# Products of ones on TensorE before the data arrive, later loads for three small tables, and the sum of squares on VectorE in a decoder layer

## The chip, the cores and the metric

The kernel runs on one core of one Trainium2 chip. The metric is device time in microseconds (us) of one execution. A core has TensorE (PE: matrix products, with its weight loads listed apart as PEld), VectorE (DVE), ScalarE (ACT), GpSimd (POOL) and SyncE (SP, which here only issues transfers). Each engine works through its own list of instructions in order; an instruction that waits for another engine holds up everything behind it on its own engine.

## The reference, cut to what matters

One layer of a decoder, for a prompt of 512 tokens and eight single sample tokens. What the opening computes is this part:

```python
def rmsnorm(x, g):
    xf = xf * lax.rsqrt(jnp.mean(xf * xf, axis=-1, keepdims=True) + EPS)
    return xf * g
u = rmsnorm(x, g_mix) @ w_in
qk, conv_new = short_conv(u[..., :2 * M], conv_buf, w_conv, b_conv)
gates = u[..., G0:G0 + 2 * M_HEADS] + b_gate
ig = gates[..., :M_HEADS]
lf = jax.nn.log_sigmoid(gates[..., M_HEADS:])
```

Behind it come four mLSTM heads and four retention heads, an output projection, a cross-attention with four heads over 256 memory tokens, a SwiGLU feed-forward part and a last norm. All arithmetic is float32.

## The kernel before, in words

All 520 tokens (512 and 8) are worked on together, features on the 128 partitions: X holds eight blocks (k = 0 to 7) of 128 features by 520 tokens. A float32 product is made of three faster ones: an operand x is split into hi (x rounded, by ScalarE) and lo (x minus hi, by VectorE or GpSimd), and hi*hi, hi*lo and lo*hi are summed. `split` does this for activations (lines 191 to 195), `wload` for a chunk of weights (line 208 hi on ScalarE, line 209 lo; the set LO_ON_POOL names the chunks whose lo GpSimd makes, among them chunks 2 and 4). `mm_k` (line 223) issues the six products (three times two halves of 260 tokens) of one block k.

The opening works as the blocks of X arrive. The transfers that SP issues are, in order: the gate weights graw, X blocks 0 and 1, weight chunk 0, X blocks 2 and 3, chunk 1, X blocks 4 to 7, the table vec, the constants cst, then chunk after chunk. GpSimd issues the gate bias bg, the state m0 and, after it has cleared the tile, the selectors sel. For each block k ScalarE makes A hi (line 194) and the square of X (line 340; block 5's square is GpSimd's, line 338), VectorE makes A lo (line 195), and GpSimd adds the squares of blocks 0 to 4 (line 342); VectorE adds the rest into ssq (line 353). TensorE adds the gates' columns pg (line 345, four products a block) and the first query block pcv with weight chunk 0; behind that the first key block, also named pcv, with chunk 1. When ssq is there, TensorE sums it over the partitions (nrm, line 285), and `rsqrt_rows` makes the norm's factor r_bc (lines 273 to 278) on ScalarE and VectorE. The products were made from the tokens without the norm, and r_bc is multiplied in when they are read: up (lines 508 to 510), vm (line 532, from ppl, the value block, made with chunk 2), gu (line 400).

Behind the opening the mixer runs its blocks query, key, value of one head after the other, each of 48 products into one of two PSUM buffers, with the conv (cv, line 518) on VectorE. Between them run the gates: gl and gu from pg, transposes pgt (line 406), VectorE's gt, u, ng (lines 412 to 428), transposes pig and plf (line 435), the scans m_r and b_r (lines 439 and 444), transposes pc (line 462), and pG, a product with BG (lines 455 and 465). GpSimd fetches two tables cosr and sinr, multiplies each by r_bc (lines 779 and 780) and makes the lo of chunk 4.

The code is not the order of the instructions. A scheduler (`schedule_with_timeline_sim=True`) simulates the program while it is built and places every engine's instructions by that, so an edit in one place can move instructions elsewhere. In the changed file the lines from the edit on have numbers that differ by one to four.

Of the kernel before, what the change touches and what calls it, by code (L numbers as in the profile page):

```python
# [13 lines left out]
AF = mybir.ActivationFunctionType  # L14
ALU = mybir.AluOpType
# [8 lines left out]
P = 128  # L24
D = 1024
KB = 8
# [15 lines left out]
PAST = 4096  # L42
NEG = -1e30
LOG_EXP = "natural_log_exp_and_others"
RSQRT_SEED = float(0x5F3759DF)


# [93 lines left out]
def decoder_step(ctx: ExitStack, tc: tile.TileContext, i: dict, o: list):  # L141
    nc = tc.nc
    pe, act, dve, pool, sp = nc.tensor, nc.scalar, nc.vector, nc.gpsimd, nc.sync
# [21 lines left out]
    def ps1(name):  # L165
        return psums[-1].tile([P, 512], F32, tag="msc", name=name)

    X = main.tile([P, KB, N], F32, name="X")
# [4 lines left out]
    ssq = main.tile([P, N], F32, name="ssq")  # L173
    cst = ctab.tile([P, C_W], F32, name="cst")
    sel = ctab.tile([P, 12 * P], F32R, name="sel")
    ones = main.tile([P, P], F32, name="ones")
# [134 lines left out]
    pool.memset(gw.bitcast(F32), 0.0)  # L311
    bg = ctab.tile([P, 8], F32, name="bg")
    m0 = ctab.tile([NS, 4], F32, name="m0")
    pool.dma_start(bg, i["b_gate"].broadcast_to([P, 8]))
    pool.dma_start(m0, i["state_mlstm_m"][0])
    sp.dma_start(graw, i["w_g8"])
    for k0, k1 in ((0, 1), (1, 2)):
        sp.dma_start(X[:, k0:k1], i["x"][:, k0:k1])
# [5 lines left out]
    sp.dma_start(vec, i["vec"])  # L324
    sp.dma_start(cst, i["cst"])
    pool.memset(sel.bitcast(F32), 0.0)
    pool.dma_start(sel[:40], i["sel"][:40])
    dve.memset(ones, 1.0)
    dve.memset(eps_c, EPS)
    split(gw[:, :, :36], gw[:, :, 64:], graw[:, :, :36])  # L330
    pg, pq0 = ps2("pg"), ps2("pcv")
# [1 line left out]
    sq = []  # L333
    for k in range(KB):
        split(A[:, 0, k], A[:, 1, k], X[:, k], scale=graw[:, k, 36:37])
        sq.append(p0.tile([P, N], F32, tag="sq", name="sq0"))
        if k == 5:
            pool.tensor_tensor(sq[k], X[:, k], X[:, k], ALU.mult)
        else:
            act.activation(sq[k], X[:, k], AF.Square)  # L340
        if 0 < k < 5:
            pool.tensor_tensor(sq[0], sq[0], sq[k], ALU.add)
        for m, s in ((100, 0), (36, 1))[:: 1 if k < KB - 1 else -1]:
            for a in range(2):
                pe.matmul(
                    pg[:m, a, :H2], gw[:, k, :m], A[:, s, k, a * H2 : (a + 1) * H2],
                    start=k == 0 and s == 0, stop=k == KB - 1 and s == 0,
                )
        mm_k(pq0, w0[0], w0[1], A, k, k, k == 0, k == KB - 1)
        if k >= 6:  # L350
            mm_k(pk0, w1[0], w1[1], A, k - 6, k - 6, k == 6, False)
    for k in range(5, KB):
        dve.tensor_tensor(ssq if k == KB - 1 else sq[k + 1], sq[k], sq[k + 1] if k < KB - 1 else sq[0], ALU.add)
    norm_rows(p0)
    for k in range(2, KB):
        mm_k(pk0, w1[0], w1[1], A, k, k, False, k == KB - 1)
# [7 lines left out]
    with ExitStack() as mx:  # L364
# [136 lines left out]
        def conv_block(kb, dst, ps=None):  # L501
            ps = ps or proj(A, "pcv")
            up = tm("up")
            L0 = 3 + T
            pool.memset(up[:, 0:3], 0.0)
            sview = up[:, L0 : L0 + 4 * NS].rearrange("p (b j) -> p b j", j=4)
            pool.tensor_copy(sview[:, :, 0:3], vec[:, kb, V_BUF : V_BUF + 24].rearrange("p (b j) -> p b j", j=3))
            dve.tensor_tensor(up[:, 3 : 3 + H2], ps[:, 0, :H2], r_bc[:, :H2], ALU.mult)
            dve.tensor_tensor(up[:, 3 + H2 : L0], ps[:, 1, : T - H2], r_bc[:, H2:T], ALU.mult)
            dve.tensor_tensor(sview[:, :, 3], ps[:, 1, T - H2 : H2], r_bc[:, T:], ALU.mult)  # L510
            pool.tensor_copy(cu[:, kb, 0:3], up[:, T : T + 3])
            pool.tensor_copy(cu[:, kb, 3:].rearrange("p (b j) -> p b j", j=3), sview[:, :, 1:4])
            LO = T + 3 + 4 * (NS - 1) + 1
            wc = lambda j: vec[:, kb, V_WC + j : V_WC + j + 1]
            cv = tm("cv")
            act.activation(cv[:, :LO], up[:, 0:LO], AF.Identity, bias=vec[:, kb, V_BC : V_BC + 1], scale=wc(0))
            for j in range(1, 4):
                dve.scalar_tensor_tensor(cv[:, :LO], up[:, j : j + LO], wc(j), cv[:, :LO], ALU.mult, ALU.add)  # L518

            th = tm("th")  # L520
            act.activation(th[:, :LO], cv[:, :LO], AF.Tanh)
            if kb < 4:
                dve.scalar_tensor_tensor(dst[:, :T], th[:, :T], 1.0, cv[:, :T], ALU.add, ALU.mult)
            else:
                pool.tensor_scalar(dst[:, :T], th[:, :T], 1.0, None, ALU.add)
                pool.tensor_tensor(dst[:, :T], dst[:, :T], cv[:, :T], ALU.mult)
            dve.scalar_tensor_tensor(dst[:, T:], th[:, T + 3 : LO : 4], 1.0, cv[:, T + 3 : LO : 4], ALU.add, ALU.mult)
            step()
# [239 lines left out]
        for h in range(4):  # L768
            q, k, v = qkv_tiles(f"m{h}")
# [16 lines left out]
        for h in range(4):  # L786
            q, k, v = qkv_tiles(f"r{h}")
# [416 lines left out]
    for f in range(PLAIN, FB):  # L1204
# [7 lines left out]
        for j, (out, (wh, wl), (xh, xl)) in enumerate(zip(ps, ops, xs)):  # L1212
            for k in range(4):
                for w, x in ((wh, xh), (wh, xl), (wl, xh)):
                    pe.matmul(  # L1215
                        out, w[:, k * P : (k + 1) * P], x[:, k * H2 : (k + 1) * H2],
                        start=k == 0 and w is wh and x is xh, stop=k == 3 and w is wl,
# [31 lines left out]
    for obs in ((0, 1), *((ob,) for ob in range(2, KB - 1))):  # L1249
        pss = [ps2("pfd") for _ in obs]  # L1250
        for k0 in range(0, FB, KB):
            for ps in pss:
                hi, lo = W.get()
                for k in range(k0, min(k0 + KB, FB)):
                    for w, s in ((hi, 0), (hi, 1), (lo, 0)):
                        for a in range(2):
                            pe.matmul(  # L1257
                                ps[:, a, :H2], w[:, k - k0], ff(s, k, slice(a * H2, (a + 1) * H2)),
                                start=k == 0 and w is hi and s == 0, stop=k == FB - 1 and w is lo,
# [26 lines left out]
    for n0, n in ((0, H2), (H2, N - H2)):  # L1286
        ts = slice(n0, n0 + n)
        ps = ps2("pfd")[:, 0, :n]
        for k0 in range(0, FB, KB):
# [3 lines left out]
            for k in range(min(KB, FB - k0)):  # L1293
                for w, s in ((hi, 0), (hi, 1), (lo, 0)):
                    pe.matmul(
                        ps, w[:, k], ff(s, k0 + k, ts),
                        start=k0 + k == 0 and w is hi and s == 0, stop=k0 + k == FB - 1 and w is lo,
# [74 lines left out]
```

## Time and profile before

| | us |
|---|---|
| three runs | 882.13, 884.52, 888.44 |
| their median | 884.52 |
| the profiled execution | 884.46 |
| its span, first to last instruction | 882.7 |

So 1.8 us of the profiled execution lie outside the span. Times in the views count from the span's start. "Busy" is the time in which an engine executes; a mean or a start is taken from one profiled execution. In a row of the timeline, the bracket at the end tells how long the engine was idle before it and what ended that.

### The profile page before, as it was taken

To read this page: it belongs to the slowest core of one execution; us is meant where nothing else is said; L and a number is where in the kernel's file an instruction comes from. 1 tells how busy PE (TensorE), PEld (TensorE's weight loads), DVE (VectorE), ACT (ScalarE), POOL (GpSimd) and SP (SyncE) were. 2 spreads that over 40 slices of the span, in tenths; PEclk is the share of its full clock that TensorE was granted. 3 is DMA by queue.
4 is the path that set the end of the run, shared out by engine and by line. 5 is a ranking of instruction groups with operands and counts; after the bars stand their busy time and mean duration, and the time that the engine had idled before them with its cause. 6 is when DMAs were issued, how large, how long until landed. Compare 5 with 4: busy or idle time off the path is not lost.

```text
span 882.7 us, 16987 instructions
## 1 busy us (share of the span) xinstructions
PE 838.9 (95%) x6707; PEld 821.9 (93%) x6707; DVE 673.3 (76%) x1509; ACT 397.4 (45%) x791; POOL 182.4 (21%) x188
## 2 busy tenths in 40 slices
PE   6999999999999999999999889999999997999994
PEld 5989989999999999889999879999999997999994
DVE  5899999877786678867888897999999997222224
ACT  5455435444546354355443554554445554222221
POOL 5544432221024301424323300000000000010011
PEclk9999999999999999999999989999999998999997
DMA  8333223334235336784764112223332232233213
GB/s 270 98 97 124 83 96 121 123 100 133 94 144 195 118 129 217 254 283 135 223 215 133 66 66 73 97 96 115 122 101 96 97 120 66 84 105 94 90 43 98
DMA packets 34600, 110.56 MB, mean 125 GB/s; under 512 B 4000, under 2 KB 8480, under 8 KB 34264
## 3 DMA queue, kind: packets, MB, share of 16 engines
q1 hardware_dynamic: 28752, 96.06, 33.9%
q0 software_dynamic: 3616, 12.34, 3.9%
q10 hardware_dynamic: 2152, 1.08, 0.5%
q8 instruction: 53, 0.87, 0.4%
q14 instruction: 27, 0.22, 0.1%
HBM read 100.38 MB, written 9.07 MB: 124 GB/s over the span
## 4 chain that ended last, share of the span: by engine, by line
PE 76%; DVE 15%; DMA 3%; issue 2%; ACT 2%; POOL 1%; SPq 0%; DVEq 0%; ACTq 0%; POOLq 0%
PE pfd L1257 13%; PE pfa L1215 6%; PE pfb L1215 6%; PE pcq L223 5%; PE pgt L223 4%; PE pwc L223 4%; PE ppl L223 4%; PE pfg L223 3%; PE pfc L1215 3%; PE pwo L223 3%; PE pfe L1215 3%; PE prp L223 3%; PE pfd L1215 3%; PE pfu L223 2%; DVE cv L518 2%
## 5 line engine op out<-in xcount | busy, mean ns | idle before, releaser
L208 ACT CAST whi<-wraw 128x1024 fp32r<-128x1024 f32 (+1 forms) x104 | 107.2, 1032 | 185.4 <-PE pfd L1257 69.6
L209 DVE TENSOR_TENSOR wlo<-wraw,whi 128x1024 fp32r<-128x1024 f32 (+1 forms) x85 | 108.9, 1282 | 74.9 <-ACT whi L208 72.9
L302 POOL TENSOR_TENSOR ssq<-ssq,sq 128x520 f32<-128x520 f32 x18 | 29.3, 1628 | 371.8 <-ACT sq L301 366.6
L191 ACT CAST qhi<-wsum 128x512 fp32r<-128x512 f32 x72 | 42.9, 619 | 54.1 <-DVE wsum L1175 45.7
L1257 PE MATMUL pfd<-TT,whi 128*128 128x260 f32 x392 | 62.8, 282 | 0.0
L209 POOL TENSOR_TENSOR wlo<-wraw,whi 128x1024 fp32r<-128x1024 f32 x19 | 46.0, 2419 | 67.7 <-ACT whi L208 62.6
L1215 PE MATMUL pfa<-TT,qhi 128*128 128x260 f32 x288 | 53.8, 284 | 0.0
L1257 PEld LDWEIGHTS pfd<-TT,whi 128*128 128x128 f32 x392 | 53.7, 188 | 0.0
L1215 PE MATMUL pfb<-TT,qhi 128*128 128x260 f32 x288 | 53.0, 283 | 0.0
L192 DVE TENSOR_TENSOR qlo<-wsum,qhi 128x512 fp32r<-128x512 f32 x72 | 47.9, 687 | 0.0
L223 PE MATMUL pwc<-B,whi 128*128 128x260 f32 x256 | 43.8, 287 | 3.6 <-DVE X L291 3.0
L223 PE MATMUL ppl<-A,whi 128*128 128x260 f32 x256 | 46.4, 295 | 0.6 <-DVE up L510 0.6
L223 PE MATMUL pcv<-A,whi 128*128 128x260 f32 x256 | 45.6, 294 | 1.1 <-ACT whi L208 1.1
L1215 PEld LDWEIGHTS pfb<-TT,qhi 128*128 128x128 f32 x288 | 44.5, 188 | 0.0
L1215 PEld LDWEIGHTS pfa<-TT,qhi 128*128 128x128 f32 x288 | 44.4, 188 | 0.0
L223 PE MATMUL pgt<-A,whi 128*128 128x260 f32 x256 | 44.0, 287 | 0.0
L223 PE MATMUL prp<-A,whi 128*128 128x260 f32 x256 | 43.8, 287 | 0.0
L1257 PE MATMUL pfd<-A,whi 128*128 128x260 f32 x224 | 37.3, 290 | 6.0 <-DVE gu L1226 6.0
L223 PE MATMUL pcq<-A,whi 128*128 128x260 f32 x256 | 42.0, 283 | 0.0
L1215 PE MATMUL pfa<-TT,qlo 128*128 128x260 f32 x144 | 40.9, 284 | 0.6 <-DVE qlo L192 0.6
L223 PE MATMUL pwo<-B,whi 128*128 128x260 f32 x256 | 41.3, 283 | 0.0
L1215 PE MATMUL pfb<-TT,qlo 128*128 128x260 f32 x144 | 40.8, 283 | 0.0
(435 smaller groups left out, 2625.4 us busy)
## 6 DMA issues: line engine op xcount, KB each, us to landing
wraw<-in_weights_dram SPq DMA_DIRECT2D x132, 512.0 KB, 3.7
kv<-in_cache_k_dram SPq DMA_DIRECT2D x16, 512.0 KB, 4.3
kv<-in_cache_v_dram SPq DMA_DIRECT2D x16, 512.0 KB, 4.3
wraw<-in_weights_dram SPq DMA_DIRECT2D x8, 384.0 KB, 3.1
X<-in_x_dram SPq DMA_DIRECT2D x2, 1040.0 KB, 6.0
Cs<-in_state_C_dram POOLq DMA_DIRECT2D x4, 512.0 KB, 5.1
out_dram<-Cs POOLq DMA_DIRECT2D x4, 512.0 KB, 3.4
Ss<-in_state_S_dram POOLq DMA_DIRECT2D x4, 512.0 KB, 3.9
```

Source lines behind the costliest of these rows:

```text
L191: act.copy(hi, src)
L192: dve.tensor_tensor(lo, src, hi.bitcast(F32), ALU.subtract)
L208: act.copy(hi[:, :n], raw[:, :n])
L209: (pool if index in LO_ON_POOL else dve).tensor_tensor(lo[:, :n], raw[:, :n], hi[:, :n].bitcast(F32), ALU.subtract)
L223: pe.matmul(ps[:m, a, :H2], w[:, k, c0 : c0 + m], x[:, s, xk, a * H2 : (a + 1) * H2], start=first and w is hi and s == 0, stop=last and w ...
L302: (dve if ob == KB - 1 else pool).tensor_tensor(ssq, ssq, s, ALU.add)
L518: dve.scalar_tensor_tensor(cv[:, :LO], up[:, j : j + LO], wc(j), cv[:, :LO], ALU.mult, ALU.add)
L1215: pe.matmul(out, w[:, k * P : (k + 1) * P], x[:, k * H2 : (k + 1) * H2], start=k == 0 and w is wh and x is xh, stop=k == 3 and w is wl,)
L1257: pe.matmul(ps[:, a, :H2], w[:, k - k0], ff(s, k, slice(a * H2, (a + 1) * H2)), start=k == 0 and w is hi and s == 0, stop=k == FB - 1 and ...
```

## The change

It puts ten products of a 128x128 tile of ones with itself at the head of TensorE's work (nothing reads the result), for which the tile of ones is filled first on VectorE. It moves the loads of bg and m0 from GpSimd to SP, behind cst, and the load of sel to GpSimd's work on the first conv block. It gives block 5's square to ScalarE and all seven additions of squares to VectorE, in a running sum as the squares come, so that GpSimd has none.

```diff
--- before.py
+++ after.py
@@ -42,6 +42,7 @@
 PAST = 4096
 NEG = -1e30
 LOG_EXP = "natural_log_exp_and_others"
+WARM = 10
 RSQRT_SEED = float(0x5F3759DF)
 
 
@@ -311,8 +312,10 @@
     pool.memset(gw.bitcast(F32), 0.0)
     bg = ctab.tile([P, 8], F32, name="bg")
     m0 = ctab.tile([NS, 4], F32, name="m0")
-    pool.dma_start(bg, i["b_gate"].broadcast_to([P, 8]))
-    pool.dma_start(m0, i["state_mlstm_m"][0])
+    dve.memset(ones, 1.0)
+    warm = ps1("warm")[:, :P]
+    for _ in range(WARM):
+        pe.matmul(warm, ones, ones, start=True, stop=True)
     sp.dma_start(graw, i["w_g8"])
     for k0, k1 in ((0, 1), (1, 2)):
         sp.dma_start(X[:, k0:k1], i["x"][:, k0:k1])
@@ -324,8 +327,8 @@
     sp.dma_start(vec, i["vec"])
     sp.dma_start(cst, i["cst"])
     pool.memset(sel.bitcast(F32), 0.0)
-    pool.dma_start(sel[:40], i["sel"][:40])
-    dve.memset(ones, 1.0)
+    sp.dma_start(bg, i["b_gate"].broadcast_to([P, 8]))
+    sp.dma_start(m0, i["state_mlstm_m"][0])
     dve.memset(eps_c, EPS)
     split(gw[:, :, :36], gw[:, :, 64:], graw[:, :, :36])
     pg, pq0 = ps2("pg"), ps2("pcv")
@@ -334,12 +337,9 @@
     for k in range(KB):
         split(A[:, 0, k], A[:, 1, k], X[:, k], scale=graw[:, k, 36:37])
         sq.append(p0.tile([P, N], F32, tag="sq", name="sq0"))
-        if k == 5:
-            pool.tensor_tensor(sq[k], X[:, k], X[:, k], ALU.mult)
-        else:
-            act.activation(sq[k], X[:, k], AF.Square)
-        if 0 < k < 5:
-            pool.tensor_tensor(sq[0], sq[0], sq[k], ALU.add)
+        act.activation(sq[k], X[:, k], AF.Square)
+        if k:
+            dve.tensor_tensor(ssq if k == KB - 1 else sq[0], sq[0], sq[k], ALU.add)
         for m, s in ((100, 0), (36, 1))[:: 1 if k < KB - 1 else -1]:
             for a in range(2):
                 pe.matmul(
@@ -349,8 +349,6 @@
         mm_k(pq0, w0[0], w0[1], A, k, k, k == 0, k == KB - 1)
         if k >= 6:
             mm_k(pk0, w1[0], w1[1], A, k - 6, k - 6, k == 6, False)
-    for k in range(5, KB):
-        dve.tensor_tensor(ssq if k == KB - 1 else sq[k + 1], sq[k], sq[k + 1] if k < KB - 1 else sq[0], ALU.add)
     norm_rows(p0)
     for k in range(2, KB):
         mm_k(pk0, w1[0], w1[1], A, k, k, False, k == KB - 1)
@@ -509,6 +507,8 @@
             dve.tensor_tensor(up[:, 3 + H2 : L0], ps[:, 1, : T - H2], r_bc[:, H2:T], ALU.mult)
             dve.tensor_tensor(sview[:, :, 3], ps[:, 1, T - H2 : H2], r_bc[:, T:], ALU.mult)
             pool.tensor_copy(cu[:, kb, 0:3], up[:, T : T + 3])
+            if kb == 0:
+                tc.keep_in_program_order(pool.dma_start(sel[:40], i["sel"][:40]))
             pool.tensor_copy(cu[:, kb, 3:].rearrange("p (b j) -> p b j", j=3), sview[:, :, 1:4])
             LO = T + 3 + 4 * (NS - 1) + 1
             wc = lambda j: vec[:, kb, V_WC + j : V_WC + j + 1]
```

What the scheduler makes of it differs from the order before over the opening and the whole mixer. Three places follow.

TensorE where pg ends and the norm's sum nrm stands. Before, 86 products precede and include the last of pg and 93 precede nrm:

```order
L345 MATMUL pg<-A,gw 36x260 x2
L345 MATMUL pg<-A,gw 100x260 x2
L223 MATMUL pcv<-A,whi 128x260 x4
L223 MATMUL pcv<-A,wlo 128x260 x2
L223 MATMUL pcv<-A,whi 128x260
L285 MATMUL nrm<-ssq,ones 128x260 x2
L223 MATMUL pcv<-A,whi 128x260 x3
L223 MATMUL pcv<-A,wlo 128x260 x2
```

Now it is 111 and 115, the ten products of ones not counted:

```order
L345 MATMUL pg<-A,gw 36x260 x2
L345 MATMUL pg<-A,gw 100x260 x2
L224 MATMUL pcv<-A,whi 128x260 x2
L224 MATMUL pcv<-A,wlo 128x260 x2
L286 MATMUL nrm<-ssq,ones 128x260 x2
L224 MATMUL pcv<-A,wlo 128x260
L224 MATMUL pcv<-A,whi 128x260 x4
L224 MATMUL pcv<-A,wlo 128x260 x2
L224 MATMUL pcv<-A,whi 128x260 x4
L224 MATMUL pcv<-A,wlo 128x260 x2
L224 MATMUL ppl<-A,whi 128x260 x4
L224 MATMUL ppl<-A,wlo 128x260 x2
```

More of the key block's products moved ahead of pg's end and of nrm; 13 of them are left behind nrm, where 35 were.

TensorE where the gates' transposes pgt stand among the 48 products of ppl. Before, after 24 of them, and 75 products lie between pgt and pig:

```order
L223 MATMUL ppl<-A,whi 128x260 x4
L223 MATMUL ppl<-A,wlo 128x260 x2
L406 MATMUL pgt<-cst,gu 128x36 x4
L406 MATMUL pgt<-cst,gu 8x36
L223 MATMUL ppl<-A,whi 128x260 x4
L223 MATMUL ppl<-A,wlo 128x260 x2
```

Now after all 48, and 52 products lie between pgt and pig:

```order
L224 MATMUL ppl<-A,whi 128x260 x4
L224 MATMUL ppl<-A,wlo 128x260 x2
L404 MATMUL pgt<-cst,gu 128x36 x4
L404 MATMUL pgt<-cst,gu 8x36
L224 MATMUL pcv<-A,whi 128x260 x4
L224 MATMUL pcv<-A,wlo 128x260 x2
```

The transposes moved back by 24 products, while pig stays at its place (234 products precede it before, 235 now). Further on, pc moved from 287 to 285, and pG from 318 to 295, so that 2 products lie between pc and pG where 23 lay.

GpSimd around the two tables that it multiplies by r_bc. Before:

```order
L511 COPY cu<-up 128x3
L779 TENSOR_TENSOR cosr<-cosr,r_bc 128x520
L780 TENSOR_TENSOR sinr<-sinr,r_bc 128x520
L512 COPY cu<-up 128x24
L209 TENSOR_TENSOR wlo<-wraw,whi 128x1024
```

Now:

```order
L509 COPY cu<-up 128x3
L511 DMA sel<-in_sel_dram 40x1536
L779 TENSOR_TENSOR cosr<-cosr,r_bc 128x520
L210 TENSOR_TENSOR wlo<-wraw,whi 128x1024
L780 TENSOR_TENSOR sinr<-sinr,r_bc 128x520
```

The issue of sel came in ahead, and the lo of chunk 4 moved between the two tables. On VectorE the lo of chunk 3 moved from behind up into the middle of the norm's factor, and vm from behind the gates' first operations to ahead of gt.

## Rows read from the trace of the kernel before

**Rows 1.** The page's first line.
```profile
span 882.7 us, 16987 instructions
```

**Rows 2.** Chain that ended last, 0 to 60 us: start, us, what.
```profile
2.60 8.40 DMA X<-in_x_dram
...
12.56 2.17 PE pcv L223 x10
...
24.05 0.88 PE nrm L285 x4
24.94 4.18 PE pcv L223 x35
...
31.99 0.41 PE pgt L406 x5
...
33.40 2.71 DVE u L422
...
38.41 2.28 DVE u L427
```

**Rows 3.** Timeline of TensorE, 0 to 14 us: start, us, instruction, idle before.
```profile
5.03 1.44 PE L345 MATMUL pg<-A,gw 128*100 128x260 f32 x4 [5.03 <-ACT A L194]
7.40 1.45 PE L345 MATMUL pg<-A,gw 128*100 128x260 f32 x4 [0.93 <-ACT A L194]
9.99 1.24 PE L223 MATMUL pcv<-A,whi 128*128 128x260 f32 x4 [1.14 <-ACT whi L208]
11.81 0.76 PE L345 MATMUL pg<-A,gw 128*100 128x260 f32 x2 [0.58 <-ACT A L194]
```

**Rows 4.** Timeline of TensorE, 30 to 60 us.
```profile
42.31 0.60 PE L435 MATMUL pig<-cst,gt 128*4 128x128 f32 x4 [0.74 <-DVE lm L474]
...
49.89 0.22 PE L462 MATMUL pc<-cst,b_r 4*128 4x4 f32 x1 [1.15 <-DVE b_r L444]
...
51.14 1.21 PE L223 MATMUL ppl<-A,whi 128*128 128x260 f32 x4 [0.60 <-DVE up L510]
```

**Rows 5.** Busy us by stretch: length, PE, PEld, DVE, ACT, POOL, granted clock, DMA share, GB/s.
```profile
11.00:14.00 3.00, 2.42 (x12) 2.20 (x11) 2.03 (x3) 2.85 (x5) 1.49 (x2) 1.00 1.04 344
...
48.00:51.00 3.00, 1.40 (x15) 1.10 (x13) 3.00 (x8) 0.66 (x1) 1.51 (x1) 1.00 0.49 164
51.00:54.00 3.00, 2.86 (x13) 2.89 (x14) 3.00 (x8) 2.41 (x4) 2.03 (x4) 0.52 0.00 0
...
60.00:100.00 40.00, 38.35 (x317) 37.51 (x317) 38.33 (x98) 19.78 (x56) 22.51 (x28) 1.00 0.30 101
```

**Rows 6.** Transfers, 9 to 12 us: total, and the packets of GpSimd's queue.
```profile
DMA packets 208, 0.78 MB, mean 259 GB/s; under 512 B 36, under 2 KB 36, under 8 KB 208
...
q0 software_dynamic: 54, 0.21, 31.0%
```

**Rows 7.** Transfers, 13 to 16 us: total.
```profile
DMA packets 416, 1.24 MB, mean 412 GB/s; under 512 B 47, under 2 KB 175, under 8 KB 416
```

**Rows 8.** Transfers issued from 0 to 20 us: KB, median us to landing.
```profile
sel<-in_sel_dram POOLq DMA_DIRECT2D x1, 240.0 KB, 8.4
```

**Rows 9.** Timeline of ScalarE, 7 to 27 us.
```profile
8.90 1.04 ACT L208 CAST whi<-wraw 128x1024 fp32r<-128x1024 f32 x1 [1.02 <-DMA wraw<-in_weights_dram]
...
23.24 0.59 ACT L398 COPY gl<-pg 36x520 f32<-36x520 f32 x1 [4.25 <-PE pg L345]
```

**Rows 10.** Timeline of all engines, 0 to 60 us: VectorE's sum of squares.
```profile
22.63 0.70 DVE L353 TENSOR_TENSOR ssq<-sq,sq 128x520 f32<-128x520 f32 x1
```

**Rows 11.** Timeline of GpSimd, 0 to 110 us.
```profile
12.43 3.02 POOL L342 TENSOR_TENSOR sq<-sq,sq 128x520 f32<-128x520 f32 x2 [3.14 <-ACT sq L340]
...
24.86 2.40 POOL L209 TENSOR_TENSOR wlo<-wraw,whi 128x1024 fp32r<-128x1024 f32 x1 [5.68 <-ACT whi L208]
...
33.47 1.31 POOL L779 TENSOR_TENSOR cosr<-cosr,r_bc 128x520 f32<-128x520 f32 x1
34.75 1.29 POOL L780 TENSOR_TENSOR sinr<-sinr,r_bc 128x520 f32<-128x520 f32 x1
```

## The prediction

> **What bounds the kernel now.** I read the chain that ended last first, for the opening: it runs over the landing of X blocks 2 and 3 at 11.00 us (2.60 + 8.40) and from there over TensorE without a gap until the norm's sum nrm at 24.05, the key block behind it and the transposes pgt at 31.99; then over VectorE, with two of its tiny operations (u, 128x20) standing at 2.71 and 2.28 us [rows 2]. So up to 11 us the opening waits for data, then TensorE's amount of work sets the time, and from 32 us on VectorE does. The pace of TensorE comes from the same rows: ten products of 260 columns in 2.17 us at 12.56, 0.217 us each, which is the level of 1.2 GHz; 35 in 4.18 us at 24.94, 0.119 us each, the level of 2.4 GHz. The column of the granted clock reads 1.00 in 11 to 14 us as well [rows 5], against that pace, so in the opening I go by the pace. Second, TensorE's timeline: before 11.81 it does four products, waits 0.93 us, four more, waits 1.14, four more, waits 0.58 [rows 3]. Third, its waits later on: 0.74 us at pig, 1.15 at pc, 0.60 at the next ppl [rows 4]; behind these two last ones the granted clock is 0.52, the 1.2 GHz level, in 51 to 54 us [rows 5]. From 60 to 100 us VectorE is busy 38.33 of 40 us [rows 5], so what it is late with at 60 us stays late.
>
> **The change part by part**, against the profiled execution (884.46 us, 0.06 below the median of the three runs; the span 882.7 lies in it [rows 1]).
>
> *Products of ones.* A product of float32 with 260 columns takes 0.44 us at the full level (nrm, four records for two products, 0.88 us [rows 2]); one of 128 columns is 0.44 x 128 / 260 = 0.22, at the half level 0.43, ten of them 4.3 us. They start when the tile of ones is filled, about 1 us into the span, and end near 5.3; the first products on data began at 5.03 [rows 3], so these come at most 0.3 us later, hidden by the wait behind them. Do they leave the clock at 2.4 GHz for the stretch after 11 us? Between them and 11 us lie the same gaps as before, longer ones if the products run at the full pace. The nearest case in the trace: waits of 1.15 and 0.60 us with eight tiny transposes between them, and the half level from 51 us [rows 4, 5]. The opening has three such gaps in a row, so I take it that the clock is back at 1.2 GHz when the work gets dense, and count 0 for the ten products; the other end is rival A.
>
> The Trainium skill, TensorE: Matmul & The Clock Gate (Rules for kernel authors), advises warming up with matmuls and makes only longer idle gaps than these responsible for a falling clock. By that the sum would be rival A's; the fall at 51 us, behind gaps of 1.15 and 0.60 us, speaks against it, so I follow the row.
>
> *Loads.* sel is 240 KB, in flight 8.4 us [rows 8]. With its packets under way the transfers moved 259 GB/s, of which GpSimd's queue 0.21 MB, in 9 to 12 us, and 412 GB/s without it in 13 to 16 [rows 6, 7]. SP's queue thus got 0.57 MB in 3 us, which takes 1.4 us at 412: 1.6 us lost, about 1.2 of it before X blocks 2 and 3 were there at 11.00. They come at about 9.8. ScalarE is in the hi of chunk 0 until 9.94 (8.90 + 1.04 [rows 9]); before, TensorE's product came 0.81 us after the landing (11.81 - 11.00 [rows 2, 3]), now 0.81 after 9.94: 10.75, 1.06 us earlier. At 0.217 us that is 5 products of lead, worth 5 x 0.119 = 0.6 us. Bounds: 0 (the transfers stay as late) to 1.06 (all at half pace). bg and m0 are needed at gt, 20 us after they can land; the two issues delay only chunk 2, whose hi stands behind gl on ScalarE.
>
> The Trainium skill, DMA: Bandwidth & Descriptors (Issuing engines are not separate DMA queues), says that transfers of all issuers interleave on the same engines. By that alone sel costs its bytes, 0.24 MB / 412 GB/s = 0.6 us, and the product would come at 11.2; rows 6 show more than that.
>
> *Squares.* VectorE gets four additions more, 4 x 0.70 = 2.8 us [rows 10], ScalarE one square; GpSimd's five operations go, and with them their hold on VectorE. Before, ssq was ready at 23.33 (22.63 + 0.70) and nrm began at 24.05 [rows 2, 10]. I cost this at 0, since TensorE now comes to nrm 2.0 us later (next step): that cover of 2.7 us hides even the whole 2.8 but 0.1. Without it the cost lies between -1 and +2.8.
>
> *Order of TensorE's products.* This is the part that costs. 115 products stand ahead of nrm, 93 before: 22 x 0.119 = 2.6, less the lead of 0.6: nrm at 24.05 + 2.0 = 26.05. The end of pg moves by 25 products: 3.0 - 0.6 = 2.4, so gl, at 23.24 before [rows 9], begins at 25.6. Chunk 2's lo hangs on gl through ScalarE's order (gl, hi, then GpSimd's lo): before it ended at 27.26 (24.86 + 2.40 [rows 11]), 4.0 us behind gl's start; now at 29.65. TensorE does nrm until 26.95, its 13 products until 28.5, four of ppl until 29.0, and waits 0.65 us, where there was no wait; 44 more, 5.25 us, end at 34.9. There pgt stands now: 34.9 to 35.3, before 31.99 to 32.40. The norm's factor is no later than that: from nrm's end (24.94) to pgt it took at most 7.05 us, with chunk 3's lo (1024 columns; 520 take 0.70 [rows 10], so some 1.4) that is 35.4 at the latest, half a microsecond behind TensorE at most, and I take 34.9. The gates begin 2.9 us later.
>
> *Gates.* From pgt's end to pig it took 42.31 - 32.40 = 9.9 us [rows 2, 4]. 4.6 of these are the two u (2.71 and 2.28) beyond some 0.2 us each, my estimate for 20 columns where 520 take 0.70; both stood while GpSimd worked (cosr and sinr without a break, 33.47 to 36.04 [rows 11]). Without any such hold it is 5.3, with vm (0.7) ahead of gt 6.0; with both holds 10.6. TensorE has 52 products, 6.2 us, to do in between (75, 8.9, before). So its wait at pig is 0 to 4.4 us. In the new order the lo of chunk 4 and sinr follow each other on GpSimd, 2.4 + 1.3 = 3.7 us; that pair is like cosr and sinr, which held VectorE for all of their time but the start: I take 2.9. Chain 8.9, pig at 44.2, before 42.31: +1.9, a wait of 2.7 us.
>
> *After that.* The scans stand ahead of the convs on VectorE, so pc does not wait (-1.15); but pG comes 2 products behind pc and waits for BG, and the next ppl for up, which now stands behind both. I take these waits and the fall of the clock there as equal to before: 0, with ends at -3.2 (1.15 + 0.60 saved, and the 1.4 us that the 0.52 of 51 to 54 us costs) and +3. Over the rest of the mixer rows change places too; no row prices that, and I give it 0, plus or minus 2.
>
> Sum: 884.46 + 1.9 = 886.4; since the clock may rise somewhat sooner after an earlier start, I say 886.0.
>
> **Rivals.** A, faster: the clock stays at 2.4 GHz from the products of ones on. Then from 10.75 the 93 products left of the 115 take 11.1 us: nrm at 21.9, 2.1 us earlier than before; chunk 2's lo at 25.4 (gl at 21.4), pgt's end at 31.2, pig at 31.2 + 8.9 = 40.1, 2.2 us earlier; 882.3, and with the waits and the fall at 51 us gone (-3.2) 879. I say 881. For it: the order fits such a pace, nrm meeting ssq; against it: the fall in rows 5. B, slower: the wait at pig is so long that the clock falls there. It decides once VectorE is held over both GpSimd operations and the wait passes some 3 us: pig at 35.3 + 10.6 = 45.9 instead of 42.31 (+3.6), 1.4 for the half level behind it, and the +3 at pG and ppl: 892.5. For it: the 2.71 us of u; against it: the two additions at 12.43 took 3.02 us where cosr and sinr took 2.57 [rows 11], as if VectorE had come in between them. C, the change does nothing in the end: TensorE gets as much from the freed VectorE as the later pg costs, and the sum stays at 884.5.
>
> **How the numbers follow.** Forecast 0.42, A 0.25, B 0.13, C 0.20. A measurement of this kernel tells 1% from no change, 8.8 us: below 875.7 there is only A with luck in the mixer (0.03), above 893.3 only B with bad luck (0.05), so 0.92 lie within. The range goes from A's lower end, 879, to 891.5, a little short of B; the forecast's own is 883 to 889.
>
> **What would show it.** Right: products at 0.217 us apart still at 12 to 14 us; the X blocks landing near 9.8; nrm near 26 with VectorE idle ahead of gl; pgt near 35; a wait of TensorE at pig of 2 us or more, none at pc, one at pG. Wrong: a pace of 0.119 from 11 us on, nrm near 22, no wait at pig.

## The result, and the profile after

The kernel after takes 897.31 us in the median of six executions (894.14 to 897.68), the kernel before 885.16 in the same comparison (882.13 to 888.44, six): ratio 1.013, 95% interval 1.0103 to 1.0157, so 11.5 us or 1.3% slower. The forecast was 886.0, and its range ended at 891.5. The profiled execution took 896.97 us; its span, against [rows 1]:

```profile
span 895.1 us, 17026 instructions
```

TensorE's timeline of the kernel after (start, us, instruction, in brackets the idle time before it and what ended it), with what answers to [rows 3, 4] and two places behind them:

```profile
1.06 4.63 PE L318 MATMUL warm<-ones 128*128 128x128 f32 x20 [1.06 <-DVE eps_c L332]
5.35 1.58 PE L345 MATMUL pg<-A,gw 128*100 128x260 f32 x6
...
9.80 1.23 PE L224 MATMUL pcv<-A,whi 128*128 128x260 f32 x4 [2.13 <-ACT whi L209]
10.84 0.69 PE L345 MATMUL pg<-A,gw 128*100 128x260 f32 x2
...
24.18 1.04 PE L286 MATMUL nrm<-ssq,ones 128*128 128x260 f32 x4
...
27.96 0.51 PE L224 MATMUL ppl<-A,wlo 128*128 128x260 f32 x2 [0.69 <-POOL wlo L210]
...
33.40 0.47 PE L404 MATMUL pgt<-cst,gu 36*128 36x36 f32 x5
...
44.28 1.01 PE L433 MATMUL pig<-cst,gt 128*4 128x128 f32 x4 [3.97 <-DVE lm L472]
...
53.41 0.40 PE L463 MATMUL pG<-BG,ones 4*128 4x32 f32 x2 [0.69 <-DVE BG L453]
...
100.68 0.33 PE L651 MATMUL ph<-cst,hs 128*128 128x128 f32 x1 [1.83 <-DVE hs L645]
...
294.38 0.70 PE L847 MATMUL pmn<-msq,ones 128*128 128x256 f32 x2 [1.55 <-POOL msq L844]
```

Against before, the norm's sum nrm is 0.3 us later (24.18 - 23.89), pgt 1.5 (33.40 - 31.92) and pig 2.0 (44.28 - 42.31 [rows 4]), which is the shift that was forecast for pig. The wait at pig is 3.97 us instead of 0.74. At ph, the transposes near 98 us, before waits 0.71 us; after waits 0.99 us at the first of them (98.39) and another 1.83 us at the second, the one shown. Busy time by stretch in the same profile (length, busy us and instructions of TensorE, its weight loads, VectorE, ScalarE, GpSimd, then the granted clock, the share of the DMA engines, GB/s), against [rows 5]:

```profile
6.50:9.50 3.00, 0.86 (x4) 0.34 (x4) 1.30 (x2) 1.22 (x2) 0.00 (x0) 1.00 0.99 365
10.00:13.00 3.00, 3.00 (x14) 2.96 (x15) 3.00 (x5) 3.00 (x5) 0.00 (x0) 0.50 1.04 421
13.50:24.00 10.50, 10.50 (x90) 10.42 (x89) 6.50 (x12) 4.53 (x9) 0.00 (x0) 1.00 0.44 166
44.00:47.00 3.00, 2.72 (x13) 2.17 (x14) 2.56 (x10) 0.82 (x4) 1.50 (x4) 0.50 0.28 22
54.20:60.60 6.40, 5.08 (x23) 4.68 (x23) 5.94 (x15) 1.64 (x4) 4.40 (x6) 0.50 0.70 213
102.00:105.00 3.00, 3.00 (x16) 3.00 (x15) 2.04 (x5) 1.57 (x3) 0.45 (x4) 0.50 0.39 152
296.50:299.50 3.00, 3.00 (x16) 3.00 (x15) 1.40 (x4) 0.32 (x1) 0.00 (x0) 0.50 0.49 173
```

Two things are to be seen. First, the opening: the granted clock is 1.00 (the 2.4 GHz level) behind the ones and still in 6.5 to 9.5 us, where TensorE is busy for 0.86 of 3 us; behind that it is 0.50 (1.2 GHz) in 10 to 13 us, and 1.00 again from 13.5 us on. Before, TensorE did only 16 records in 13.5 to 16.5 us, though the column reads 1.00 there, so for before's opening the pace tells the level and not the column:

```profile
13.50:16.50 3.00, 3.00 (x16) 2.92 (x16) 2.65 (x3) 2.73 (x4) 2.92 (x3) 1.00 1.04 416
```

Second, behind the waits at pig, at pG and the next ppl, at ph and at pmn it is at 0.50 while TensorE is busy: 13 to 16 records take 3 us there, and in the stretches at the full level that are shown below 24 to 28 are done in 3 us.

VectorE and GpSimd in the kernel after, first VectorE's timeline, then GpSimd's [rows 10, 11]:

```profile
19.30 0.69 DVE L342 TENSOR_TENSOR ssq<-sq,sq 128x520 f32<-128x520 f32 x1
...
36.48 5.18 DVE L518 SCALAR_TENSOR_TENSOR cv<-up,vec,cv 128x544 f32<-128x544 f32 x1 [0.79 <-ACT cv L516]
...
43.21 0.17 DVE L426 SCALAR_TENSOR_TENSOR gt<-gt,u 128x20 f32<-128x20 f32 x1
...
98.05 2.97 DVE L645 TENSOR_SCALAR hs<-hs,hny 128x128 f32<-128x128 f32 x4
```

```profile
36.15 1.33 POOL L779 TENSOR_TENSOR cosr<-cosr,r_bc 128x520 f32<-128x520 f32 x1
37.44 2.39 POOL L210 TENSOR_TENSOR wlo<-wraw,whi 128x1024 fp32r<-128x1024 f32 x1
39.79 1.28 POOL L780 TENSOR_TENSOR sinr<-sinr,r_bc 128x520 f32<-128x520 f32 x1
41.02 0.70 POOL L512 COPY cu<-up 128x24 f32<-128x24 f32 x1
...
98.20 2.35 POOL L210 TENSOR_TENSOR wlo<-wraw,whi 128x1024 fp32r<-128x1024 f32 x1
```

A step of the convolution (cv), 0.79 us by itself (the next two take 0.78 and 0.79), takes 5.18: it ends 0.6 us behind the third of three GpSimd operations that follow each other (41.66 against 41.07). The gates' gt stands behind it on VectorE, and pig is made from gt; the bracket at pig names lm, which follows gt on VectorE by 0.8 us. At 98 us four scalings (hs) take 2.97 us beside one lo of GpSimd. In the kernel before the same four take 0.88, since that lo starts 1 us behind them. VectorE's timeline of before at that place:

```profile
94.04 0.88 DVE L645 TENSOR_SCALAR hs<-hs,hny 128x128 f32<-128x128 f32 x4
```

and GpSimd's:

```profile
95.82 0.19 POOL L511 COPY cu<-up 128x3 f32<-128x3 f32 x1 [1.66 <-DVE up L509]
95.97 2.41 POOL L209 TENSOR_TENSOR wlo<-wraw,whi 128x1024 fp32r<-128x1024 f32 x1
```

The lists say why. GpSimd's list at this place, before and then after: the lo has changed places with the copy cu, which waits for VectorE.

```
L633 MEMSET hs_1780 128x5
L707 MEMSET d_1673 128x5
L511 COPY cu<-up 128x3
L209 TENSOR_TENSOR wlo<-wraw,whi 128x1024

L633 MEMSET hs_1791 128x5
L707 MEMSET d_1684 128x5
L210 TENSOR_TENSOR wlo<-wraw,whi 128x1024
L509 COPY cu<-up 128x3
```

Where the time goes, by the starts of seven first products in two profiles of each kernel (the second ones are d4 and d3 below), in us; pfg belongs to the feed-forward part, pn to the last norm:

| | nrm | pgt | pig | ph | pmn | pfg | pn |
|---|---|---|---|---|---|---|---|
| before | 23.89 | 31.92 | 42.31 | 94.38 | 287.89 | 495.05 | 860.92 |
| before again | 23.47 | 31.50 | 40.99 | 92.99 | 286.21 | 495.03 | 860.54 |
| after | 24.18 | 33.40 | 44.28 | 98.39 | 294.38 | 504.69 | 873.50 |
| after again | 22.47 | 31.69 | 42.56 | 97.03 | 292.77 | 502.94 | 868.65 |

By the means of each pair, pn is 10.3 us later. Of this 1.8 us are there at pig; 2.3 come from pig to ph, 2.5 from ph to pmn, 2.3 from pmn to pfg, 1.6 from there to pn. The wait of 1.83 us at ph falls into the stretch from ph to pmn, since it stands ahead of the second ph.

### The profile page after: what moved, and what is told of

Same layout as the page of the kernel before. It is cut to its first block, busy times and chain, and to the rows that moved or that the text cites. A ratio compares the mean times of both kernels' runs of the same rounds, so it can differ in the third digit from the quotient of the medians.

```text
span 895.1 us, 17026 instructions
## 1 busy us (share of the span) xinstructions
PE 849.0 (95%) x6727; PEld 831.4 (93%) x6727; DVE 673.0 (75%) x1513; ACT 397.5 (44%) x792; POOL 177.4 (20%) x181
## 4 chain that ended last, share of the span: by engine, by line
PE 71%; DVE 16%; DMA 6%; issue 3%; ACT 2%; POOL 1%; SPq 0%; DVEq 0%; ACTq 0%; POOLq 0%
PE pfd L1257 13%; PE pgt L224 5%; PE pcq L224 5%; PE pwo L224 5%; DMA wraw<-in_weights_dram 4%; PE pwc L224 4%; PE pfa L1215 4%; PE pfb L1215 4%; PE ppl L224 3%; PE pfg L224 3%; PE prp L224 3%; PE pcv L224 2%; PE pfu L224 2%; DVE qlo L193 2%; PE pfe L1215 2%
## 5 line engine op out<-in xcount | busy, mean ns | idle before, releaser
L224 PE MATMUL pwo<-B,whi 128*128 128x260 f32 x256 | 42.4, 288 | 0.0
```

Of the source, the lines that this page charges most:

```text
L224: pe.matmul(ps[:m, a, :H2], w[:, k, c0 : c0 + m], x[:, s, xk, a * H2 : (a + 1) * H2], start=first and w is hi and s == 0, stop=last and w ...
```

## The experiments

Theory O: the ten ones cost it, because the scheduler counts them in and writes other lists for all engines. Rivals: the squares' sums on VectorE (S), the moved loads (L), the ones' own work on TensorE (W).

**a1 to a4: one part each.** a1 is after with `WARM = 0`; the others put one part into before (the lines added; those that they replace are the ones of the change's diff):

```diff
 a2  +    dve.memset(ones, 1.0)
     +    warm = ps1("warm")[:, :P]
     +    for _ in range(10):
     +        pe.matmul(warm, ones, ones, start=True, stop=True)
 a3  +    sp.dma_start(bg, i["b_gate"].broadcast_to([P, 8]))
     +    sp.dma_start(m0, i["state_mlstm_m"][0])
     ...
     +            if kb == 0:
     +                tc.keep_in_program_order(pool.dma_start(sel[:40], i["sel"][:40]))
 a4  +        act.activation(sq[k], X[:, k], AF.Square)
     +        if k:
     +            dve.tensor_tensor(ssq if k == KB - 1 else sq[0], sq[0], sq[k], ALU.add)
```

a1: 

> The kernel after without the ten products of ones; the earlier loads and the squares on VectorE stay. Theory O (the ones cost the time: by them the gates' product pgt stands behind the value projection, its chain meets three GpSimd operations in a row, pig waits 3.97 us and the clock falls there): the wait at pig is under 2 us, no half-level stretch between 40 and 48 us, the time 884 to 889 us. Theory S (the squares' sums on VectorE cost it): stays at 894 to 898. Theory L (the moved loads cost it, the selectors' issue in the gates' stretch): stays at 894 to 898. Theory D (the later clock falls at 101.8, 296 and 753.7 us come by themselves and not from the opening): some of them stay and the time is 888 to 893.

a2: 

> The kernel before with the ten products of ones alone. Theory O: 893 to 898 us, a wait of 3 to 5 us at pig. Theory S and theory L: 883 to 887. Theory D: 888 to 893, with later clock falls that before does not have.

a3: 

> The kernel before with the loads alone moved (bias, state and selectors behind X, the selectors' issue at the first convolution). Theory O and theory S: 883 to 887 us, X complete about 1 us earlier. Theory L: 893 to 898. Theory D: 884 to 893.

a4: 

> The kernel before with the squares alone changed (all on ScalarE, their sums on VectorE). Theory O and theory L: 883 to 887 us. Theory S: 893 to 898. Theory D: 884 to 893.

Measured, as the ratio to before with its interval: a1 1.0023 (1.0003 to 1.0044), a2 1.0148 (1.0108 to 1.0188), a3 1.0007 (0.9984 to 1.0031), a4 1.0030 (1.0010 to 1.0050). The ones alone, with the lists that the scheduler then writes, cost as much as the whole change; S and L fall. But a2 waits only 1.54 us at pig, not 3 to 5, and loses its time elsewhere, so O is right on the part and not on the one place. a1 misses O's rows too: it waits 2.45 us at pig, and its clock is at the half level from 42.4 to 45.8 us, where I had expected none; still it is only 2.0 us above before.

**b1 to b4: the lists held fast.** Do the ones cost by the lists or by themselves? In these kernels a table holds every engine's instructions in a given order; the edges move no data:

```diff
     with tile.TileContext(nc, schedule_with_timeline_sim=True) as tc:
         decoder_step(tc, args, outs)
+        hold_order(tc)
...
+        for a, b in zip(order, order[1:]):
+            tc.add_manual_dep(
+                row[int(b)], row[int(a)].name,
+                mybir.DependencyInfo(mybir.DependencyClass.NoSync, mybir.DependencyReason.DATA), reason="order",
+            )
```

b1: 

> The kernel before with the ten products of ones at the head, and every engine's list held in the order that before has (a table of the order, laid over the program as edges that move no data). The ones alone cost 13 us with an order of their own. Theory P (the scheduler counts the ones, so it packs and orders all the later lists otherwise, and the new lists cost the time): 881 to 886 us here, and a clock at the high level from about 6 us. Theory W (the ones themselves cost it, by what they do to TensorE's clock later in the program): 893 to 898.

b2: 

> The kernel after without the ones, every engine's list held in the order that after has. Theory P: 894 to 900 us, with the wait of about 4 us at pig and the clock at half after it. Theory W: 884 to 888.

b3: 

> The kernel after, ones included, every engine's list held in the order of a1_no_ones. Theory P: 883 to 887 us. Theory W: 894 to 898. If both play: 888 to 893.

b4: 

> The kernel of a3_loads_only with the ones, every engine's list held in the order of a3_loads_only: the candidate that may beat both kernels. Theory P: 880 to 884 us, by X about 1 us earlier and the opening's products at the high level. Theory W: 893 to 898.

Measured: b1 1.0029 (1.0009 to 1.0049), b2 1.0056 (1.0024 to 1.0088), b3 1.0050 (1.0028 to 1.0071), b4 1.0053 (1.0032 to 1.0073). Neither theory alone holds: b1, b2 and b4 lie between the two, and b3 where I had put it if both play. At before's lists the ones lose most of their cost (b1 against a2), and after's lists without the ones are slower than a1's, by 2.9 us (1.0056 against 1.0023). b2 shows that the waits of after up to ph come from its lists, not from the ones' work; TensorE's timeline of b2:

```profile
44.29 1.01 PE L435 MATMUL pig<-cst,gt 128*4 128x128 f32 x4 [3.92 <-DVE lm L474]
...
101.06 0.33 PE L653 MATMUL ph<-cst,hs 128*128 128x128 f32 x1 [1.84 <-DVE hs L647]
```

The same waits at the same times. But the ones at equal lists still cost 2.4 us (b3 against a1), 2.6 (b1 against before), 4.1 (b4 against a3) and 6.5 (after, 1.0130, against b2). The intervals part in the last two pairs; those of b3 and a1 overlap, as do those of b2 and a1, and b1's clears 1 by 0.0009. In the first three pairs the kernel with the ones has the table of the order and the other has not. No run holds a kernel's own lists and changes nothing else, so what the table itself costs is not measured; c4 below, held and without ones, is within 0.5 us of a3 by the ratios. In b1's profile the ones first gain: pig at 40.38 without a wait, pmn at 287.00. The loss comes from pmn to pfg, among other things where VectorE's kf waits for an output of its buffer to land:

```profile
364.05 0.42 DVE L884 TENSOR_TENSOR kf<-pmk,rm_bc 128x256 f32<-128x256 f32 x1 [2.04 <-DMA out_dram<-kf]
```

This kf waits so in three other profiles with ones (b4, c2 and d2, 1.35 to 2.28 us) and in no other, neither in before nor in the two of after, so it is not what after loses.

**c1 to c4: what in the lists.** c1 takes the multiplies of cosr and sinr out of GpSimd's row at the gates, c2 puts 17 products ahead of pig, c3 gives TensorE the list of a1, c4 is a3 with the edit of c1:

```diff
 c1 (GpSimd's list)
-L779 TENSOR_TENSOR cosr<-cosr,r_bc 128x520
 L210 TENSOR_TENSOR wlo<-wraw,whi 128x1024
-L780 TENSOR_TENSOR sinr<-sinr,r_bc 128x520
...
 L663 TENSOR_TENSOR Cs<-Cs,fib 128x1024
 L512 COPY cu<-up 128x24
+L779 TENSOR_TENSOR cosr<-cosr,r_bc 128x520
+L780 TENSOR_TENSOR sinr<-sinr,r_bc 128x520
 c2
+            for _ in range(17):
+                pe.matmul(pig[:, :P], ones, ones, start=True, stop=True)
             for a, out in enumerate((pig, plf)):
```

c1: 

> The kernel after in its own order on every engine, but for two GpSimd operations: the multiplies of cosr and sinr stand behind the second state's work (about 66 us) instead of around chunk 4's lo at 36 to 41 us. Theory H (the three GpSimd operations in a row hold VectorE's cv for 5.18 us, so pig waits 3.97 us and the clock falls there): cv is held some 2.5 us less, pig's wait is 1 to 2 us, the clock does not fall at 43.75, and the time is 3 to 6 us below after, 891 to 894 by the same before. Theory T (TensorE's own list costs it, wherever VectorE stands): within 1.5 us of after.

c2: 

> The kernel after in its own order, with 17 more products of ones put on TensorE just ahead of pig (3.6 us at the high level, in the wait of 3.97 us). Theory C (what the wait costs is the clock that falls behind it): no half-level stretch at 43.75, the lag to before at 60 us about 2 us smaller, the time 2 to 4 us below after. Theory I (the wait costs by its own length, the clock little): within 1.5 us of after.

c3: 

> The kernel after with TensorE's list as in a1_no_ones (behind the ones) and the four other engines' lists as in after. Theory T: 4 to 8 us below after, 888 to 892. Theory H: the hold of VectorE stays, and the time stays within 2 us of after.

c4: 

> The kernel of a3_loads_only in its own order, with the multiplies of cosr and sinr moved on GpSimd to the idle stretch at about 73 us: no ones, X early, no long hold of VectorE at the gates. By theory H pig's wait (1.41 us there) goes, and the time is 1 to 3 us below a3_loads_only, 880 to 883: a candidate to beat both kernels. By theory T no change, 883 to 885.

c1: 1.0113 (1.0083 to 1.0144), 1.5 us below after's 1.013 by the ratios, whose intervals overlap. The rows are as theory H has them, the time is at the end of theory T's 1.5 us. VectorE of c1, then TensorE, then stretches:

```profile
34.21 2.68 DVE L520 SCALAR_TENSOR_TENSOR cv<-up,vec,cv 128x544 f32<-128x544 f32 x1 [0.79 <-ACT cv L518]
```

```profile
39.51 0.60 PE L435 MATMUL pig<-cst,gt 128*4 128x128 f32 x4 [1.40 <-DVE lm L474]
...
96.70 0.48 PE L653 MATMUL ph<-cst,hs 128*128 128x128 f32 x1 [1.84 <-DVE hs L647]
```

```profile
40.00:43.00 3.00, 3.00 (x27) 2.93 (x26) 3.00 (x7) 1.95 (x5) 0.85 (x1) 1.00 0.35 102
96.50:99.50 3.00, 2.80 (x12) 2.56 (x13) 2.03 (x8) 1.44 (x3) 0.57 (x5) 0.50 0.60 160
```

The hold is 2.5 us shorter, the wait at pig 2.6, the clock stays up behind it, and ph comes at 94.41, as in before. Then the wait at ph, with the clock at half behind it, takes the gain back.

c2: 1.0146 (1.0122 to 1.0170), not faster. It doesn't tell C from I: the 17 products waited with pig and started at 44.01, behind the same 3.96 us, so they fill nothing and put the transposes of pig to 49.37, 5.1 us later than in after. In this profile the delay doesn't reach the end: ph is 3.7 us later than in after, pn 0.7 earlier, and no half level came at 296 or 740 us. Against d3, the second profile of after, pn is 4.1 us later, so no rule can be read from it.

c3: 1.0298 (1.0268 to 1.0328), 15 us above after by the ratios. Both theories miss, T by its sign: TensorE's list isn't good or bad by itself. With the others' lists against it, TensorE waits 6.5 us at ph and 3.3 at pmn between 90 and 320 us. c4: 1.0012 (0.9990 to 1.0035), the same as a3, though the hold of 5.36 us in a3 is gone and TensorE no longer waits at pig (1.41 us there): theory H's 1 to 3 us don't come, and this is no kernel that beats both. So a long hold ahead of pig need not cost anything at the end.

**d1 to d4: the ones' amount, and second profiles.** d1 and d2 are b1 with `range(2)` and `range(24)`; d3 and d4 are after and before without an edit.

d1: 

> The kernel before with two products of ones at the head and every list as before has it. If the ones' cost at equal lists (2.6 us with ten) comes from their work on TensorE, two of them cost under 1 us: 883 to 886 us. If it comes from any change of the program at its head (another place of a buffer, a longer list of instructions), they cost the same 2 to 4 us: 886 to 889.

d2: 

> The kernel before with 24 products of ones at the head, which keep TensorE busy until about 9 us, and every list as before has it. If the ones' work costs by its amount: 888 to 892 us. If the cost does not depend on it: 886 to 889. If the clock held high through the opening is worth something: 882 to 885, with the first stretch at the high level not broken at 9 us.

d3: 

> The kernel after once more, for a second profile. The waits that belong to its lists come again: about 4 us at pig, 0.7 at ppl, 1.8 at ph near 100 us, with half-level stretches at 44 and 54. The half-level stretches near 102, 296 and 740 us come again if they belong to the lists, and some are gone or elsewhere if each depends on where it falls in that execution. 894 to 898 us.

d4: 

> The kernel before once more, for a second profile. The waits come again (0.7 at pig, 1.6 at pmn near 288 us, 1.2 at ph near 123 us). If half-level stretches behind waits of 1 to 2 us fall differently in every execution, one or two stand elsewhere than at 51, 495, 512 and 737 us. 881 to 888 us.

d1: 1.0026 (0.9998 to 1.0054); d2: 1.0047 (1.0020 to 1.0074). Two ones cost about as much as ten (1.0029), and 24 may cost more, within the intervals; so it is likely not the amount of their work, but d1's interval still holds 1, and this isn't shown. In d2 the clock stays at the high level from the ones on and gains nothing: nrm starts at 23.60, as in before, and in 10 to 13 us TensorE has 2.13 us of work.

d3 took 891.35 us, below all six executions of the result (before stood at 883.49 in its comparison), d4 883.55. In d4 the half level comes from 50, 494, 511 and 736 us, in the same places as in before (51, 495, 512 and 737), while the waits are other ones (none at pig, 0.46 us at pmn for 1.62). In d3, TensorE and then stretches:

```profile
42.56 0.80 PE L433 MATMUL pig<-cst,gt 128*4 128x128 f32 x3 [3.96 <-DVE lm L472]
...
99.32 0.33 PE L651 MATMUL ph<-cst,hs 128*128 128x128 f32 x1 [1.83 <-DVE hs L645]
...
292.77 0.70 PE L847 MATMUL pmn<-msq,ones 128*128 128x256 f32 x2 [1.92 <-POOL msq L844]
```

```profile
10.00:13.00 3.00, 2.92 (x24) 2.89 (x25) 3.00 (x6) 3.00 (x6) 0.00 (x0) 1.00 1.03 404
42.40:45.40 3.00, 2.84 (x14) 2.27 (x15) 2.56 (x9) 0.94 (x4) 1.50 (x4) 0.50 0.12 15
100.40:103.40 3.00, 3.00 (x14) 3.00 (x15) 1.99 (x6) 1.57 (x3) 0.51 (x4) 0.50 0.43 164
295.00:298.00 3.00, 3.00 (x27) 3.00 (x27) 2.72 (x6) 1.63 (x3) 0.00 (x0) 1.00 0.41 164
```

The waits at pig and ph and the half level behind them come again, as they do in b2: they belong to the lists. The half level near 740 us comes again at 735, the one behind pmn does not, though the wait there is longer (1.92 against 1.55 us). And here the clock never fell in the opening; nrm was 1.7 us earlier than in the first profile, and the end still 7 us later than before's.

**e1 and e2: the pair at ph.** e1 swaps the two rows in after's list that the section on the result shows; e2 does that and the move of c1.

```diff
 L707 MEMSET d_1684 128x5
-L210 TENSOR_TENSOR wlo<-wraw,whi 128x1024
 L509 COPY cu<-up 128x3
+L210 TENSOR_TENSOR wlo<-wraw,whi 128x1024
```

e1: 

> The kernel after in its own lists, but for one swap on GpSimd: the lo at about 98 us stands behind the copy cu, as it does in before. Theory G (GpSimd's lo holds VectorE's hs, TensorE waits for it at ph and the clock falls there): hs takes 0.9 us instead of 2.97, the wait of 1.83 us at ph is gone or under 0.5, no half-level stretch at 100 to 106, and the time is 2.5 to 4.5 us below after. Rival R (what is saved there comes back behind it, in other waits or stretches at the half level): the same rows at ph, but the time within 1.5 us of after.

e2: 

> The kernel after in its own lists with both GpSimd edits: cosr and sinr behind the second state's work (as in c1_hold_away) and the lo behind cu (as in e1_lo_behind_cu). Theory G: 4 to 8 us below after, 887 to 891 us, at the level of b1 and b3 (1.003 to 1.005 of before). Rival R: 892 to 895, as c1_hold_away alone.

e1: 1.0124 (1.0094 to 1.0155); e2: 1.0075 (1.0047 to 1.0102). VectorE's row in e2, TensorE's, and the stretches behind pig and ph:

```profile
97.20 0.88 DVE L647 TENSOR_SCALAR hs<-hs,hny 128x128 f32<-128x128 f32 x4
```

```profile
42.47 0.60 PE L435 MATMUL pig<-cst,gt 128*4 128x128 f32 x4 [1.45 <-DVE lm L474]
...
97.54 0.33 PE L653 MATMUL ph<-cst,hs 128*128 128x128 f32 x1 [0.73 <-DVE hs L647]
```

```profile
42.60:45.60 3.00, 3.00 (x27) 2.85 (x26) 3.00 (x6) 2.25 (x6) 1.20 (x3) 1.00 0.21 70
100.20:103.20 3.00, 3.00 (x28) 3.00 (x27) 2.96 (x4) 0.47 (x2) 2.16 (x4) 1.00 0.27 40
```

e1 alone is the rival's: the row at ph is mended (hs 0.88) and the time isn't, within what can be told. Both together take after from 1.0130 to 1.0075, 4.9 us, a little short of theory G's 887 to 891 (891.9). From ph to pmn e2 takes 192.9 us, before 193.5 and 193.2, after 196.0 and 195.7. So the two places at which GpSimd's new list holds VectorE are some two fifths of the loss, by ratios whose intervals only just part (up to 1.0102 and from 1.0103). One edit alone gave 1.5 us (c1), the other 0.5 (e1); that they give more together is not explained.

No kernel tried beats before; a3, with the loads alone, c4 and d1 can't be told from it.

## Why the prediction was wrong

*Ones: 0 for themselves.* They start at 1.06 and the first products on data come 0.3 us later than before, as forecast. The clock too: in the profile of after it is at half from 10 to 13 us; in d3 it was not, and that is rival A's opening (nrm at 22.47, A had 21.9). A's gain did not follow. The sentence that the forecast takes from the Trainium skill, TensorE: Matmul & The Clock Gate, stands there in the section Why this matters for your kernels; by it waits of under 2 us would not matter, and here the clock fell behind 1.83 us at ph and 1.55 us at pmn. What this term left out is that products at the head, two or 24 of them, come with 2.3 to 6.5 us at equal lists, though b1's profile is ahead of before's up to pmn; why, no run shows.

*Loads.* Right: the dense work began at 10.84 (forecast 10.75). The transfers moved in 9 to 12 us, against 259 GB/s [rows 6]:

```profile
DMA packets 379, 1.22 MB, mean 406 GB/s; under 512 B 45, under 2 KB 103, under 8 KB 379
```

By the Trainium skill, DMA: Bandwidth & Descriptors (Issuing engines are not separate DMA queues), sel would have cost its bytes alone, and the work have begun at 11.2 (the forecast's estimate); it began at 10.84, so here the trace speaks for more. *Squares: 0.* Covered as forecast, ssq being ready at 19.99, 4.2 us ahead of nrm; yet a4 stands 2.7 us above before, with lists of its own, so the 0 holds for the additions and not for what the scheduler makes of them.

*Order, up to pig: +1.9.* Right in its sum by luck, since two errors cancel. I let the pace of 1.2 GHz last until 17 us as before; in after it ended at 13, so that nrm came 0.3 us later, not 2.0, in spite of the 22 products more ahead of it, and pgt came at 33.40 instead of 34.9. Then the gates' chain from pgt's end (33.87) to pig took 10.4 us, not 8.9: VectorE was held over the lo and sinr, and the rest of cosr as well, near the 10.6 of rival B. The wait of 0.69 us at ppl came as forecast (0.65).

*After that: 0, with ends at -3.2 and +3; the rest of the mixer 0, plus or minus 2.* This is the step that failed. From pig to pn before takes 818.6 and 819.6 us, after 829.2 and 826.1: 8.6 us in the mean, where the forecast had none. TensorE in these stretches, before, d4, after and d3:

```profile
42.31:860.92 818.61, 794.98 (x6393) 781.20 (x6394) 632.08 (x1438) 371.54 (x745) 154.21 (x145) 0.99 0.38 123
40.99:860.54 819.55, 794.93 (x6396) 780.84 (x6395) 633.12 (x1437) 371.60 (x745) 154.41 (x145) 0.99 0.39 123
44.28:873.50 829.22, 802.86 (x6393) 787.41 (x6394) 632.79 (x1437) 370.56 (x744) 157.66 (x145) 0.98 0.38 121
42.56:868.65 826.09, 799.86 (x6393) 785.07 (x6393) 633.09 (x1437) 371.06 (x744) 156.99 (x145) 0.98 0.38 121
```

The products are the same. TensorE's idle time grows by 2.2 us in the mean, its busy time by 6.4: three quarters of the loss are the same products done more slowly, and a quarter is waiting. The clock's records have 33.6 and 30.4 us at the half level in these stretches of after and 20.5 in both of before; half of that difference, 5.8 us, is an estimate of what it costs. So what failed is above all the term of the clock: the forecast's sum counted one fall, at the ppl near 51 us, as equal to before, and gave none to pig or to any later wait. The half level that before does not have stands behind pig (0.50 in 44 to 47 us; this is rival B's fall, since the wait passed the 3 us at which I had let B decide); behind pG and ppl, where it lasts 6.8 us and in before 3.4; behind ph, whose wait of 1.8 us comes from a swap on GpSimd's list at 98 us; and, in the first profile alone, behind pmn. The forecast's steps end at the ppl near 55 us; for the rows that change places behind it, it said that no row prices them. But GpSimd's list showed the swap, and the two u of before gave the price of such a hold [rows 2]. B was the rival that came about at pig; its 892.5 priced the gates alone.

What adds up, by ratios: loads and squares 2.0 us (a1), after's lists 2.9 (b2 against a1), the ones at after's lists 6.5 (after against b2). These make up the 11.5 us, but the last of them is more than the 2.4 to 4.1 us that the ones cost at other lists, and it rests on how executions spread: d3 is 6 us below the median of after, b2's seven lie at 887.5 to 888.4 (four) and 892.2 to 896.0 (three), and in their profiles b2 and d3 take nearly the same time from pig to pn (825.4 and 826.1 us). In e2 the three executions at 887.6 to 888.0 us have a mean granted clock of 0.980 to 0.984, the five at 891.8 to 893.8 one of 0.976 to 0.978. So part of the cost is how often the clock falls in an execution, and what the ones do to that at equal lists stays open.

## What to carry to other kernels

Where a scheduler orders all engines by a modelled time, work added "for nothing" to one engine rewrites every list. So compare the lists of the engines that seem idle, all the way, and look for long GpSimd operations that now start beside VectorE work which TensorE waits for. Then compare not only TensorE's waits but its busy time on the same products, which shows what the clock took behind them. Or hold the old lists fast and add the work to them, which here cost 2.6 us where the free scheduler made it 13. A gain in the opening is worth what arrives at the first stage that waits for something else, and a second profile of the same kernel tells which stages to believe.

## What the runs showed of the hardware

- A VectorE operation that meets GpSimd's can be held over several of them: 5.18 us beside three in a row, 2.68 beside one, 0.79 alone. The Trainium skill, SBUF — State Buffer (SBUF: two separate sides), calls the port pair that the two engines share an exclusive lock, held for a whole instruction; the trace agrees. It shows too that the waiting cv did not come in between the three, but did ahead of the small copy cu behind them, which took 0.70 us where the next one took 0.20.
- Behind the same wait the clock falls in one execution and not in another: 1.55 us at pmn with the half level behind it, 1.92 us without. The Trainium skill, TensorE: Matmul & The Clock Gate (What's actually happening), says that the gate's window does not start with the kernel and that the moment of a change differs from run to run; these two profiles fit that.
- In the 13 profiles with ones the stretch from pmn to pfg takes 209.3 to 212.2 us, in the 7 without them 207.2 to 209.3. Take off TensorE's idle time in it and half of its time at the half level, and 201.9 to 202.8 us are left in all 20, so these two explain the difference. TensorE is idle there for 5.6 to 8.3 us with ones and 4.9 to 6.0 without. Why it waits longer with ones, also where the lists are the same (b1 and before), stays open.
